# Spreading the late sort passes, making both offsets first, larger groups and narrower clears in a gather, transform and scatter kernel

## The chip, the cores and the metric

The kernel runs on one core of one Trainium2 chip. The metric is the device time of one execution in microseconds. A kernel was run three times or more in its comparison, beside runs of the kernel before on the same chip. A run is called slow when it is over 1.5% above the fastest of the same kernel; only fast runs enter a ratio. Times inside a trace count from the start of the span, which is about 1.7 us shorter than the measured time.

The engines are called PE (the matrix engine), DVE (the vector engine), ACT (the scalar engine) and GpSimd or POOL. PEld is PE's weight load.

## The reference

```python
# nodes 4096 x 256, edges 262144, both weights 256 x 256
self_out = nodes @ w_self
msg = nodes[edges_src] @ w_msg
agg = np.zeros((N, D)); np.add.at(agg, edges_dst, msg)
return self_out + agg
```

## The kernel before

The kernel does not gather rows. It sorts the edges on the chip and then counts, with matrix products of one-hot tiles, how often each pair of source and destination occurs in a narrow band; the counts, multiplied with Y = nodes @ w_msg, give the sums. Until about 164 us it loads and sorts. Then come 2048 chunks of 128 edges. The sort of the second half of the chunks is not finished by then: 32 operations on XL, here called the passes, are done on DVE in between.

For a group of chunks, mostly 64, DVE makes two one-hot tiles, e (128 wide) and d (W = 110 wide). For each it subtracts once (the offset, two inputs, 1024 elements in each partition) and then compares this offset with constants: eight comparisons for e, seven for d.

```python
for nm, val, wid, row in (("e", slo_b, P, jrow), ("d", rel_b, W, drow)):
    o = ohp.tile([P, 32, wid, 2], BF16, name=nm + "_oh", tag=nm, bufs=3)
    ...
        u = ohp.tile([P, 32, JB, 2], I16, name=nm + "_off", tag="off", bufs=2)
        tt(out=u[...], in0=v..., in1=row..., op=ALU.subtract)         # the offset
        for j in range(0, wid, JB):                                   # JB = 16
            w = min(JB, wid - j)
            tss(out=o[:, 0:n // 2, j:j + w, :], in_=u[:, 0:n // 2, 0:w, :],
                scalar=float(-j), op=ALU.is_equal)                    # one comparison
```

PE then counts each chunk with one matmul into a bank of a ring of six in PSUM. A run is one bank filled: it is cleared at both ends by a matmul with zeros, counted into, copied to SBUF by ACT (`atr`), and applied. The last 110 columns of a run belong to its successor. For five of six pairs of runs GpSimd starts a DMA that adds them there (a merge; 163 issues in all, as some merges are split in two). LAG = 46 chunks after its evacuation PE applies the run, and that matmul has to wait for the merge.

```python
def merge(r):
    i, j = r % NAT, (r + 1) % NAT
    ...
        nc.gpsimd.dma_start(
            out=atr[:, b:b + n, 0:W], in_=atr[:, a:a + n, SW:SW + W], accum_op=ALU.add)

def apply_run(r):
    ...
    for t in range(NT):
        nc.tensor.matmul(out=out_ps[:, t, :], lhsT=at[:, t * P:(t + 1) * P], rhs=Y[:, b, :], ...)

    # for each chunk c:
            while nev < NRUN and (evac_at(nev) <= c or c == NCOL - 1):
                evac(nev)
                if nev % 2 == 0 and nev and by_dma(nev - 1):
                    merge(nev - 2)
                todo.append((c + LAG + (SWITCH if nev % NB == 0 else 0), nev))
                ...
            while todo and (todo[0][0] <= c or c == NCOL - 1):
                apply_run(todo.pop(0)[1])
```

## Time and profile before

| Kernel before | |
|---|---|
| median of 3 runs | 481.92 us (481.26 to 483.63) |
| span of the profiled run | 478.6 us |
| busy share PE, DVE, ACT, GpSimd | 79%, 87%, 50%, 41% |
| PE starts chunk 960 | 320.23 us |
| PE starts chunk 2047 | 467.43 us |

```profile
244.54 1.19 POOL L501 DMA_DIRECT2D atr<-atr  x1 [0.26 <-ACT atr L481]
246.21 3.29 POOL L501 DMA_DIRECT2D atr<-atr  x3 [0.48 <-ACT atr L481]
```

d_off begins 0.08 us before the last e comparison ends (244.00 + 2.65 = 246.65), but the d comparisons begin 0.03 us after d_off ends (246.57 + 0.68 = 247.25), because they read it. The three merge issues that started at 246.21 overlap one another and were through 3.29 us later. The longest of all 163 took 1.90 us.

### The profile page before, as it was taken

To read this page: it belongs to the slowest core of one execution; us is meant where nothing else is said; L and a number is where in the kernel's file an instruction comes from. 1 tells how busy PE (TensorE), PEld (TensorE's weight loads), DVE (VectorE), ACT (ScalarE), POOL (GpSimd) and SP (SyncE) were. 2 spreads that over 40 slices of the span, in tenths; PEclk is the share of its full clock that TensorE was granted. 3 is DMA by queue.
4 is the path that set the end of the run, shared out by engine and by line. 5 is a ranking of instruction groups with operands and counts; after the bars stand their busy time and mean duration, and the time that the engine had idled before them with its cause. 6 is when DMAs were issued, how large, how long until landed. Compare 5 with 4: busy or idle time off the path is not lost.

```text
span 478.6 us, 10994 instructions
## 1 busy us (share of the span) xinstructions
PE 378.8 (79%) x4107; PEld 309.2 (65%) x4107; DVE 415.7 (87%) x884; ACT 240.5 (50%) x459; POOL 196.0 (41%) x190
## 2 busy tenths in 40 slices
PE   0009646999872698997887998799999999999994
PEld 0004231655451358996777987699999899999893
DVE  7999999899899999999999998999998687897400
ACT  3100010221282245775555666677776677777771
POOL 4200000000000034665554566577667676776760
PEclk9999986999997699999899899999999999999998
DMA  8794111111000013344243234444535454545451
GB/s 321 118 171 127 25 26 25 27 27 25 14 0 0 0 13 25 28 48 47 24 46 38 28 30 43 49 45 48 54 39 55 38 55 38 57 40 54 38 60 41
DMA packets 66306, 23.78 MB, mean 50 GB/s; under 512 B 52170, under 2 KB 64970, under 8 KB 66250
## 3 DMA queue, kind: packets, MB, share of 16 engines
q0 software_dynamic: 43872, 10.42, 26.8%
q1 hardware_dynamic: 21548, 10.42, 8.3%
q10 hardware_dynamic: 830, 2.20, 1.2%
q8 instruction: 34, 0.56, 0.5%
q14 instruction: 22, 0.18, 0.1%
HBM read 8.92 MB, written 6.30 MB: 32 GB/s over the span
## 4 chain that ended last, share of the span: by engine, by line
DVE 45%; PE 43%; DMA 5%; issue 3%; ACT 2%; POOL 1%; SPq 0%; DVEq 0%; ACTq 0%; POOLq 0%
PE ring L425 17%; DVE XA L749 15%; PE out_ps L524 14%; DVE e_oh L402 9%; DVE d_oh L402 8%; PE warm L786 6%; DVE XS L749 6%; DVE XL L746 4%; PE tp_sw L892 2%; DMA d<-in_edges_dst_dram 2%; DMA atr<-atr 2%; DVE d_off L396 2%; DVE e_off L396 1%; POOL atr L501 1%; PE out_ps L599 1%
## 5 line engine op out<-in xcount | busy, mean ns | idle before, releaser
L501 POOL DMA_DIRECT2D atr<-atr x163 | 187.3, 1265 | 260.0 <-ACT atr L481 257.1
L481 ACT CAST atr<-ring 128x484 bf16<-128x484 f32 x352 | 192.3, 565 | 100.9 <-PE ring L425 80.9
L425 PE MATMUL ring<-d_oh,e_oh 128*128 128x110 bf16 x2048 | 195.6, 215 | 18.4 <-DVE d_oh L402 16.2
L425 PEld LDWEIGHTS <-e_oh 128*128 128x128 bf16 x2048 | 163.8, 98 | 23.6 <-issue 13.9
L524 PE MATMUL out_ps<-Y,atr 128*128 128x256 bf16 x1056 | 171.6, 274 | 1.4 <-DMA atr<-atr 1.4
L402 DVE TENSOR_SCALAR e_oh<-e_off 128x1024 bf16<-128x1024 int16 (+1 forms) x264 | 99.6, 448 | 17.9 <-PE ring L425 15.7
L786 PE MATMUL warm<-zw 128*128 128x512 bf16 x176 | 56.0, 418 | 65.8 <-DVE XA L749 51.4
L749 DVE TENSOR_TENSOR XA<-XA 128x510 f32<-128x510 f32 (+35 forms) x142 | 97.1, 731 | 5.4 <-ACT XA L896 3.7
L524 PEld LDWEIGHTS <-atr 128*128 128x128 bf16 x1056 | 90.5, 98 | 8.2 <-DMA atr<-atr 1.9
L425 PE MATMUL ring<-zer 128*128 128x204 bf16 x352 | 88.3, 251 | 1.4 <-ACT atr L481 1.3
L402 DVE TENSOR_SCALAR d_oh<-d_off 128x1024 bf16<-128x1024 int16 (+3 forms) x231 | 86.2, 443 | 1.1
L786 PEld LDWEIGHTS <-zw 128*128 128x128 bf16 x176 | 16.7, 102 | 101.2 <-issue 55.0
L896 ACT COPY XA<-tp_sw 128x512 f32<-128x512 f32 x24 | 14.2, 592 | 92.5 <-PE tp_sw L892 91.8
L425 PEld LDWEIGHTS <-zer 128*128 128x128 bf16 x352 | 34.4, 98 | 9.8 <-issue 6.0
L749 DVE TENSOR_TENSOR XS<-XS 128x512 f32<-128x512 f32 (+17 forms) x40 | 28.9, 769 | 2.6 <-ACT XS L950 2.0
L746 DVE TENSOR_TENSOR XL<-XL 128x1196 f32<-128x1196 f32 (+15 forms) x32 | 28.1, 918 | 0.3
L892 PEld LDWEIGHTS tp_sw<-XA,id 128*128 128x128 f32 x192 | 22.5, 190 | 4.5 <-issue 2.3
L892 PE MATMUL tp_sw<-XA,id 128*128 128x128 f32 x192 | 23.8, 276 | 1.8 <-DVE XA L749 1.7
L396 DVE TENSOR_TENSOR e_off<-slo_b,jrow 128x1024 int16<-128x1024 int16 (+1 forms) x33 | 21.6, 655 | 0.0
L396 DVE TENSOR_TENSOR d_off<-rel_b,drow 128x1024 int16<-128x1024 int16 (+1 forms) x33 | 21.5, 653 | 0.0
L643 DVE COPY bsum<-ring 1x3 f32<-1x3 f32 x1 | 0.1, 149 | 24.1 <-PE ring L642 24.1
L519 PE MATMUL out_ps<-Y,atr 128*128 128x256 bf16 x65 | 17.6, 272 | 0.0
(104 smaller groups left out, 153.8 us busy)
## 6 DMA issues: line engine op xcount, KB each, us to landing
atr<-atr POOLq DMA_DIRECT2D x123, 55.0 KB, 2.8
out_dram<-o_sb SPq DMA_DIRECT2D x110, 32.0 KB, 1.6
nodes_bf<-in_nodes_dram POOLq DMA_DIRECT2D x1, 2048.0 KB, 16.1
nodes_bf_dram<-nodes_bf SPq DMA_DIRECT2D x1, 2048.0 KB
atr<-atr POOLq DMA_DIRECT2D x40, 27.5 KB, 2.8
s<-in_edges_src_dram ACTq DMA_DIRECT2D x2, 512.0 KB
d<-in_edges_dst_dram SPq DMA_DIRECT2D x2, 512.0 KB, 8.2
XT<-nodes_bf_dram SPq DMA_TRANSPOSE x64, 2.4
```

Of the source, the lines that this page charges most:

```text
L396: tt(out=u[:, 0:n // 2], in0=v.to_broadcast(shp), in1=row[:, 0:JB, :].unsqueeze(1).to_broadcast(shp), op=ALU.subtract,)
L402: tss(out=o[:, 0:n // 2, j:j + w, :], in_=u[:, 0:n // 2, 0:w, :], scalar=float(-j), op=ALU.is_equal,)
L425: mm = nc.tensor.matmul(out=ap, lhsT=lhsT, rhs=rhs, start=start, stop=True, skip_group_check=True,).ins
L481: ins = nc.scalar.copy(out=at[:, 0:SW + W], in_=ring[:, b:b + SW + W]).ins
L501: nc.gpsimd.dma_start(out=atr[:, b:b + n, 0:W], in_=atr[:, a:a + n, SW:SW + W], accum_op=ALU.add)
L519: nc.tensor.matmul(out=out_ps[:, 0, :], lhsT=spill[:, SW:SW + P], rhs=Y[:, b, :], start=False, stop=False, skip_group_check=True,)
L524: nc.tensor.matmul(out=out_ps[:, t, :], lhsT=at[:, t * P:(t + 1) * P], rhs=Y[:, b, :], start=False, stop=(b == NB - 1), skip_group_check=True,
L746: self.defer.append(lambda: self.nc.vector.tensor_tensor(out=out, in0=in0, in1=in1, op=op))
L749: self.nc.vector.tensor_tensor(out=out, in0=in0, in1=in1, op=op),
L786: self.nc.tensor.matmul(out=w[:], lhsT=self.zw[:, 0:P], rhs=self.zw[:], start=True, stop=True).ins
L892: self.nc.tensor.matmul(out=tp[:, g * P:(g + 1) * P], lhsT=self.turned(rots[8 * h + 4 * t + g]), rhs=sel(x)[:, 4 * t + g], start=True, sto ...
L896: self.nc.scalar.copy(out=sel(y)[:, 4 * t:4 * t + 4], in_=tp[:].rearrange("p (g i b) -> p g i b", g=4, b=bb),)
```

## The change

The intent is to balance two regimes. DVE sets the pace while it does the passes, and PE afterwards. The 32 passes are spread over the groups at chunks 192 to 832, two or three a group, in place of those at 256 to 704, four a group. (LATE_FROM and LATE_SUB are where they begin and where they have to be done; LATE_TURN and SHIFT place the transposes of the second half, at a chunk and at a run; LATE_USE, where its places were computed, goes.) Both offsets are made before either comparison, so that no operation reads the one right before it. Groups of 32 become groups of 64 or are compared directly. The clears become 90 columns wide at each end, with a check at the end that this sufficed.

```diff
-GAP = W - 8
+GAP = 90
-SHIFT = 148
-LATE_FROM = 256
-LATE_STEP = 4
-LATE_SUB = 768
-LATE_TURN = 872
-LATE_USE = 960
+SHIFT = 160
+LATE_FROM = 192
+LATE_SUB = 896
+LATE_TURN = 942
...
-    sizes = [8, 8, 16, 32, 32, 32] + [64] * ((NCOL - 128) // 64)
+    sizes = [8, 8, 16, 32] + [64] * 31
...     (split_at: one cut after HALF moved from 256 to 64 chunks)
...     (onehots, shortened)
+        both = []
         for nm, val, wid, row in (("e", slo_b, P, jrow), ("d", rel_b, W, drow)):
-            (offset, then its comparisons)
+            (offset only; for n <= 32 the direct comparison)
+            both.append((o, u, wid))
+        for o, u, wid in both:
+            for j in range(0, wid if u is not o else 0, JB):
+                tss(out=o[...], in_=u[...], scalar=float(-j), op=ALU.is_equal)
...     (loop over chunks)
-                if c == LATE_USE:
-                    late.places()
                 e, d = onehots(c, starts[c])
                 if c >= LATE_FROM:
-                    for _ in range(LATE_STEP):
-                        if rest:
-                            rest.pop(0)()
+                    due = len(ops) * (c + starts[c] - LATE_FROM) // (LATE_SUB - LATE_FROM)
+                    for op in ops[done:due]:
+                        op()
+                    done = max(done, min(due, len(ops)))
                 if c == LATE_SUB:
                     late.bases()
                     ...
+                    late.places()
...     (the check for the fallback: a finer test on bases and first offsets, five tiny operations more)
```

More of the change, by code (lines that the diff above doesn't have):

```diff
@@ L23 @@
 W = 110
-GAP = W - 8
+GAP = 90
 NB = 32
 JB = 16
+MAXG = 64
 HALF = 1024
-SHIFT = 148
-LATE_FROM = 256
-LATE_STEP = 4
-LATE_SUB = 768
-LATE_TURN = 872
-LATE_USE = 960
+SHIFT = 160
+LATE_FROM = 192
+LATE_SUB = 896
+LATE_TURN = 942
 NSEG = 11
@@ L373, in split_vals @@
         tss(out=rel_b[:, c0:c1], in_=vals[:, c0:c1], scalar=7, op=ALU.logical_shift_right)
-    split_at = {0: 64, 64: 512, 512: HALF, HALF: HALF + 256, HALF + 256: NCOL}
-    sizes = [8, 8, 16, 32, 32, 32] + [64] * ((NCOL - 128) // 64)
+    split_at = {0: 64, 64: 512, 512: HALF, HALF: HALF + 64, HALF + 64: NCOL}
+    sizes = [8, 8, 16, 32] + [64] * 31
     assert sum(sizes) == NCOL
     def onehots(c, n):
-        res = []
         if c in split_at:
             split_vals(c, split_at[c])
+        both = []
@@ L384, in onehots @@
         for nm, val, wid, row in (("e", slo_b, P, jrow), ("d", rel_b, W, drow)):
-            o = ohp.tile([P, 32, wid, 2], BF16, name=nm + "_oh", tag=nm, bufs=3)
+            o = ohp.tile([P, MAXG // 2, wid, 2], BF16, name=nm + "_oh", tag=nm, bufs=3)
             v = val[:, c:c + n].rearrange("p (g i) -> p g i", i=2).unsqueeze(2)
-            if n < 32:
-                shp = [P, n // 2, wid, 2]
-                tt(
-                    out=o[:, 0:n // 2], in0=v.to_broadcast(shp),
-                    in1=row[:].unsqueeze(1).to_broadcast(shp), op=ALU.is_equal,
-                )
-            else:
-                u = ohp.tile([P, 32, JB, 2], I16, name=nm + "_off", tag="off", bufs=2)
-                shp = [P, n // 2, JB, 2]
-                tt(
-                    out=u[:, 0:n // 2], in0=v.to_broadcast(shp),
-                    in1=row[:, 0:JB, :].unsqueeze(1).to_broadcast(shp), op=ALU.subtract,
-                )
-                for j in range(0, wid, JB):
-                    w = min(JB, wid - j)
-                    tss(
-                        out=o[:, 0:n // 2, j:j + w, :], in_=u[:, 0:n // 2, 0:w, :],
-                        scalar=float(-j), op=ALU.is_equal,
-                    )
@@ L406, in onehots @@
-            res.append(o)
-        return res
+            u, jb = o, wid
+            if n > 32:
+                u = ohp.tile([P, MAXG // 2, JB, 2], I16, name=nm + "_off", tag=nm + "o", bufs=2)
+                jb = JB
+            shp = [P, n // 2, jb, 2]
+            tt(
+                out=u[:, 0:n // 2], in0=v.to_broadcast(shp),
+                in1=row[:, 0:jb, :].unsqueeze(1).to_broadcast(shp),
+                op=ALU.is_equal if u is o else ALU.subtract,
+            )
+            both.append((o, u, wid))
@@ L410, in line @@
+        for o, u, wid in both:
+            for j in range(0, wid if u is not o else 0, JB):
+                w = min(JB, wid - j)
+                tss(
+                    out=o[:, 0:n // 2, j:j + w, :], in_=u[:, 0:n // 2, 0:w, :],
+                    scalar=float(-j), op=ALU.is_equal,
+                )
+        return [o for o, _, _ in both]
     def line(at, r):
@@ L553 @@
         nev = 0
-        rest = sort.late
+        ops, done = sort.late, 0
         starts = {}
@@ L562 @@
                 c0 = c
-                if c == LATE_USE:
-                    late.places()
                 e, d = onehots(c, starts[c])
                 if c >= LATE_FROM:
-                    for _ in range(LATE_STEP):
-                        if rest:
-                            rest.pop(0)()
+                    due = len(ops) * (c + starts[c] - LATE_FROM) // (LATE_SUB - LATE_FROM)
+                    for op in ops[done:due]:
+                        op()
+                    done = max(done, min(due, len(ops)))
                 if c == LATE_SUB:
-                    assert not rest
+                    assert done == len(ops)
                     late.bases()
@@ L635 @@
     tt(out=v[:], in0=gn[:], in1=gi[:], op=ALU.subtract)
-    stt(out=bad[:], in0=v[:], scalar=float(GAP), in1=bad[:], op0=ALU.is_gt, op1=ALU.add)
+    stt(out=bad[:], in0=v[:], scalar=float(W), in1=bad[:], op0=ALU.is_gt, op1=ALU.add)
+    tt(out=v[:], in0=v[:], in1=dl[:], op=ALU.add)
+    stt(out=bad[:], in0=v[:], scalar=float(SW + GAP), in1=bad[:], op0=ALU.is_gt, op1=ALU.add)
+    tss(out=v[:], in_=v[:], scalar=float(SW), op=ALU.is_ge)
+    stt(out=v[:], in0=dl[:], scalar=float(SW - GAP), in1=v[:], op0=ALU.is_lt, op1=ALU.mult)
+    tt(out=bad[:], in0=bad[:], in1=v[:], op=ALU.add)
     stt(
```

## The prediction

> **What bounds the kernel now.** I read the page's 40 slices first, then a table of busy times by stage, then the waits inside the stages, then the vector engine's timeline. Words used below: a chunk is 128 edges, one matmul into the ring; 2048 chunks are taken in groups, mostly of 64, and for each group DVE (the vector engine) makes two one-hot tiles, e and d; a run is one ring bank, cleared by a matmul, filled, evacuated and applied; the passes are the 32 sort operations on XL that prepare chunks 1024 to 2047.
>
> The 40 slices (11.97 us each):
>
> ```profile
> PE   0009646999872698997887998799999999999994
> DVE  7999999899899999999999998999998687897400
> PEclk9999986999997699999899899999999999999998
> ```
>
> Until slice 13 the kernel sorts, which the change leaves alone. From slice 14 the chunks run. Up to slice 25 DVE has a 9 everywhere and PE has sevens and eights; from slice 26 PE has nines and DVE falls. So there are two regimes. The table of busy times shows it closer (columns: stretch, its length, busy us and count of each engine, granted clock, DMA):
>
> ```profile
> core 0: us, PE busy (x) PEld busy (x) DVE busy (x) ACT busy (x) POOL busy (x), PEclk, DMA share, GB/s
> 209.00:310.00 101.00, 85.47 (x1078) 78.33 (x1076) 97.49 (x223) 61.57 (x116) 57.07 (x50) 0.97 0.40 39
> 320.00:468.00 148.00, 145.29 (x1913) 134.25 (x1911) 111.13 (x268) 107.42 (x202) 102.06 (x89) 1.00 0.48 47
> ```
>
> First row: DVE is busy 97%, PE 85%. Second row: PE 98%, DVE 75%. The waits say the same, first for 200 to 308 us, then for 310 to 450 us (us in total, times, longest):
>
> ```profile
> PE ring L425 <- DVE d_oh L402: 13.8, 8, 3.1
> DVE gn L633 <- DMA kn<-kd: 1.7, 1, 1.7
> ```
>
> ```profile
> DVE e_oh L402 <- PE ring L425: 15.7, 11, 3.4
> ```
>
> Early, PE waits for the one-hots; late, DVE waits for PE to give a one-hot buffer back. Counting the ring matmuls off the timeline: group 960 starts on PE at 320.23 us, chunk 2047 at 467.43, so 17 groups take 147.2 us, 8.66 each. DVE had group 960 ready at 316.97. The end of the program is therefore the time at which PE can start group 960 plus a stage that PE sets, plus a tail of 11.2 us (478.6 - 467.43).
>
> What DVE does before then, in its own timeline (start, us, what):
>
> ```profile
> 280.59 2.65 DVE L746 TENSOR_TENSOR XL<-XL 128x528 f32<-128x528 f32 x4
> 283.16 0.68 DVE L396 TENSOR_TENSOR e_off<-slo_b,jrow 128x1024 int16<-128x1024 int16 x1
> 283.95 2.88 DVE L402 TENSOR_SCALAR e_oh<-e_off 128x1024 bf16<-128x1024 int16 x8
> 286.75 0.68 DVE L396 TENSOR_TENSOR d_off<-rel_b,drow 128x1024 int16<-128x1024 int16 x1
> 287.46 2.88 DVE L402 TENSOR_SCALAR d_oh<-d_off 128x1024 bf16<-128x1024 int16 x7
> ```
>
> A group is 7.2 us: from e_off to the end of d_oh the 13 groups 128 to 896 took 95.4 us, less the 1.7 us wait for kn in one of them, over 13. Four passes behind a group cost another 2.5 to 5.1. So a step with passes was 9.4 to 12.6 us against PE's 8.66, and the steps without them (before chunk 256, after 704) were shorter than PE's. In the timeline an operation that reads the one just before it starts 0.11 us after its end (e_oh after e_off) or 0.03 us (d_oh after d_off); one that doesn't starts 0.08 us before the end of its predecessor.
>
> [...] 512 elements of e_oh took 309 ns, 1024 took 462 on average and about 0.35 us a step where nothing disturbed them. [...] The trace has 249 ns at 204 columns and 215 at 110, 0.36 ns a column, so 9. [...] Here the two longest pauses of PE (3.46 us from start to start before 228.1, 3.03 before 260.9) are followed by windows with a granted clock of 0.91 to 0.92 and 0.83[...].
>
> **The change, part by part.**
> 1. Spread: 32 passes go from eight groups (256 to 704, four each) to eleven (192 to 832, two or three each). The DVE work before group 960 is the same, 26.9 us of step time. What changes is who waits: DVE's steps become about 7 + 2.5 = 9.5 us, close to PE's. PE's idle gaps shrink from 3 us to about 1[...].
> 2. Offsets first: e_off, d_off, e_oh, d_oh. Two dependent starts vanish: 0.11 + 0.08 and 0.03 + 0.08, 0.30 us. Part of the 0.11 is probably the wait for the buffer, which stays, so I take 0.24 us: a group is 6.96 us.
> 3. Groups: the two groups of 32 at 64 and 96 took 9.08 us of DVE (173.92 to 183.00) and become one of 64, 6.96 us: 2.1 saved. The group of 32 at chunk 32 is now made by two direct comparisons. One over 2048 elements took 1.22 us and one over 1760 1.07; twice the elements, an estimate, 2.3 + 2.0 us, against 4.1 now. Nothing either way.
> 4. Bases, subtraction and places move together behind group 896: 2.4 + 1.5 us as before. The wait for kn (1.7 us) should vanish, as about 2.9 us of other DVE work now lies between. The wider test adds 5 tiny operations of 0.17 us, some 0.6 us with overlaps.
> 5. Clears: 352 matmuls of 180 columns in place of 204[...]. It counts only where PE is the bound: 17 groups with 11 runs each[...].
>
> Sum for DVE. Group 64 starts at 174.1 (as now, 173.92, plus 0.2). 15 groups to the end of group 960: 15 x 6.96 = 104.4. Passes 26.9, the split of values at 512 0.5, bases to places 3.9, test 0.6. 174.1 + 136.3 = 310.4; I take 311.0, as the passes' ops summed singly come out 1.2 us higher. PE: group 896 is ready at about 299.5 and takes 8.55 us plus 1.5 for the eight transposes of the late half, so it is done at 309.6 and waits for group 960 until 311.0. Before: 320.23. Gain 9.2 us. Behind it DVE's steps of about 7 are shorter than PE's 8.55, so PE stays the bound and the stage shrinks only by the clears' 1.9. Total 11.1: 481.9 - 11.1 = 470.8 us.
>
> Of the 9.2, 6.0 is DVE being done earlier (316.97 to 311.0). The other 3.2 is that PE is no longer late behind DVE there: the transposes and the slot waits of the late half, which delayed PE at 301 to 312 us (group 832 took 10.2 us), now fall in a group behind which PE would wait anyway.
>
> **The rivals.**
> A. DVE's work before group 960 is what counts, and spreading does not shrink it. If offsets-first and merging save nothing, DVE has group 960 ready at 316.97 - 1.7 + 0.6 = 315.9; the gain is 4.3 + 1.9 and the time 475.7. For it: DVE is at 97% in the stage either way. Against it: the dependent starts are plain in the timeline.
> B. PE becomes the bound over the whole stretch, as DVE's tensor_scalar steps get shorter. They range from 0.27 to 0.85 us, so some of them are held up by something. PE alone would start group 960 at 189 + 13 x 8.55 + 1.5 = 301.7, and the time would be 461.5. Against it: 6.96 + 2.5 is longer than 8.55.
> C. The late half turns late: transposes now at chunks 928 and 942, and the one-hots of 1024 need them. PE is at 942 at about 307, ScalarE takes 0.7 us, DVE asks at about 311: a slack of 3 us. If it were lost, DVE would wait, but PE still has group 960 to chew on, so it costs 0 to 3 us, up to 474.
> D. The looser test fails on these data, and the slow general path runs: far slower. I took the edges from the reference, sorted them exactly and applied the new test: largest step between neighbouring bases 96 (limit 110), largest first offset in a run 69 (limit 90), smallest last offset 298 (limit 284). The network sorts almost so; I give it 2%.
>
> **Range and chances.** DVE's group time is the large uncertainty: 0.2 us either way over 15 groups is 3 us. PE's group time of 8.55 with 0.1 either way is 1.7 us. Before's three runs scatter over 2.4 us. I take 466.5 to 475.5. The limit of 2% is 472.3, only 1.5 us from my number, so faster 0.62, same 0.36, slower 0.02.
>
> **What would show it.** Group 960 starts on PE at 309 to 313 us; DVE's e_oh follows d_off with an overlap, and a group takes about 7.0; waits of PE for d_oh many but short (under 2 us); the wait for kn gone; clears near 240 ns; 8.5 us a group after 960. The prediction is wrong if groups still take 7.2 us, if PE waits for vals, or if PE's stage after 960 grows.

For the clears it takes 1.9 us, which no trace shows. By the trace's 0.36 ns a column (249 ns at 204 columns, 215 at 110), 24 columns are 9 ns, and the 187 clears (17 groups with 11 runs each) 1.7 us.

## More of the kernel before

From the page, its slices, and the group of its merge issues (busy us, mean ns of one, then its idle time):

```profile
POOL 4200000000000034665554566577667676776760
L501 POOL DMA_DIRECT2D atr<-atr x163 | 187.3, 1265 | 260.0 <-ACT atr L481 257.1
```

From slice 16 on (slices count from 0) GpSimd is mostly 50 to 70% busy with nothing but these issues, and what ends its idle time is ACT, which has evacuated a run. This held nobody up: PE hardly ever waited for a merge. From the waits of the whole run (us in total, times, longest):

```profile
PE out_ps L524 <- DMA atr<-atr: 1.4, 3, 1.0
```

Now a stretch of the timeline, first DVE's, then GpSimd's (start, us, engine and line, operation, output and inputs, how many; in brackets the idle time before it):

```profile
244.00 2.65 DVE L402 TENSOR_SCALAR e_oh<-e_off 128x1024 bf16<-128x1024 int16 x7
246.57 0.68 DVE L396 TENSOR_TENSOR d_off<-rel_b,drow 128x1024 int16<-128x1024 int16 x1
247.28 2.44 DVE L402 TENSOR_SCALAR d_oh<-d_off 128x1024 bf16<-128x1024 int16 x7
```

The chain that ended last, by engine:

```profile
DVE 45%; PE 43%; DMA 5%; issue 3%; ACT 2%; POOL 1%; SPq 0%; DVEq 0%; ACTq 0%; POOLq 0%
```

## The result, and the profile after

The changed kernel took 487.77 us, the median of four runs (486.88 to 490.17), against 482.75 us (481.26 to 483.63, four runs) before. The ratio is 1.0115, with a 95% interval from 1.0068 to 1.0162: 1.2% slower, inside the 2% that count as the same. The result is correct. A ratio here and below is the mean time of one kernel's fast runs over that of the other's of the same rounds, so it is not quite the ratio of the medians quoted.

The slices of the page after (12.2 us each):

```profile
PE   0009636989871886978888999977999999999994
DVE  8998999899899999999968999766868779786400
POOL 4200000000000057786868666768676676776660
PEclk9999885999996798988989999998999999999998
```

DVE has lost its row of nines from 244 us on (its 21st digit), as was wanted, but PE has not gained them: it shows a 6 at 183 to 195 us and two sevens at 317 to 342 us. Of the three engines shown only GpSimd has become busier over the whole span (46% in place of 41). The busy times by stretch (columns as in the prediction's table; the first stretch is shown for this kernel, the other two answer to the rows of before):

```profile
180.00:250.00 70.00, 57.22 (x674) 51.07 (x674) 65.72 (x144) 37.23 (x68) 54.56 (x34) 0.91 0.36 32
```

```profile
209.00:310.00 101.00, 89.98 (x1113) 80.25 (x1111) 92.76 (x228) 62.11 (x117) 72.69 (x53) 0.95 0.41 40
320.00:478.00 158.00, 148.67 (x1951) 136.22 (x1949) 110.24 (x276) 111.10 (x209) 110.66 (x89) 0.99 0.45 45
```

From 209 to 310 us neither DVE (92.76 of 101) nor PE (89.98) is full now. GpSimd was busy for 72.69 us with 53 issues, before for 57.07 with 50. The number of merges is unchanged, so each takes longer:

```profile
L498 POOL DMA_DIRECT2D atr<-atr x163 | 217.6, 1620 | 239.5 <-ACT atr L478 237.1
```

The mean is 1620 ns where it was 1265, the longest 6670 where it was 1901, and 19 issues are over 2 us where none was. The waits of the whole run show who pays:

```profile
PE out_ps L521 <- DMA atr<-atr: 17.5, 10, 3.9
DVE e_oh L400 <- PE ring L422: 32.4, 18, 4.3
DVE slo_b L371 <- ACT vals L311: 7.4, 2, 6.9
PE ring L422 <- DVE d_oh L400: 1.9, 1, 1.9
```

PE's wait for one-hots has nearly gone, as intended. In its place PE waits 17.5 us for merged runs, and 10.5 of them in the stretch from 170 to 250 us. DVE, now ahead, waits for PE to give buffers back. One such wait in the timeline, for DVE, GpSimd and PE in turn:

```profile
207.59 0.68 DVE L391 TENSOR_TENSOR e_off<-slo_b,jrow 128x1024 int16<-128x1024 int16 x1
208.19 0.68 DVE L391 TENSOR_TENSOR d_off<-rel_b,drow 128x1024 int16<-128x1024 int16 x1
208.80 2.77 DVE L400 TENSOR_SCALAR e_oh<-e_off 128x1024 bf16<-128x1024 int16 x8
211.48 2.40 DVE L400 TENSOR_SCALAR d_oh<-d_off 128x1024 bf16<-128x1024 int16 x7
213.80 1.22 DVE L748 TENSOR_TENSOR XL<-XL 128x1024 f32<-128x1024 f32 x1
```

```profile
209.11 6.31 POOL L498 DMA_DIRECT2D atr<-atr  x2 [0.31 <-ACT atr L478]
```

```profile
215.87 0.39 PE L521 MATMUL out_ps<-Y,atr 128*128 128x256 bf16 x2 [2.46 <-DMA atr<-atr]
```

Each DVE line begins before the one above it ends. The fifteen comparisons are one chain without a gap from 208.80 to 213.88 us. The merge issue that begins at 209.11, 0.31 us into the chain, lasts until 214.20 (the first of the two on the line; 5.09 us alone), when the chain is over and a pass has begun. An undisturbed issue takes 1.19 us. The merge lands at 215.82, and PE, which has stood for 2.46 us, goes on at 215.87.

The chain that ended last contains GpSimd now, with 13% (before 1%), and DMAs with 8% (before 5%), of which the page puts 6% down to the merges (before 2%):

```profile
PE 43%; DVE 22%; POOL 13%; issue 10%; DMA 8%; ACT 2%; SPq 0%; POOLq 0%; DVEq 0%; ACTq 0%
```

Where the time came from is plainest in the moments at which PE starts certain chunks. The last column anticipates experiment 1, the changed kernel with the old order of offsets.

| chunk | before | after | after, old order |
|---|---|---|---|
| 192 | 198.37 | 204.04 | 199.87 |
| 448 | 239.24 | 250.83 | 236.55 |
| 896 | 311.97 | 313.74 | 302.75 |
| 960 | 320.23 | 324.92 | 315.49 |
| 1024 | 329.04 | 339.56 | 324.14 |
| 2047 | 467.43 | 477.26 | 462.55 |

By chunk 448 the changed kernel is 14.3 us behind its old-order sister. It regains 4.9 us by chunk 960 (PE has work in store while DVE is ahead) and loses 6.0 again in the group from 960 to 1024. There the late transposes, at chunk 942 on PE, come late because PE is late; DVE waits 6.9 us for `vals`, and PE then waits for DVE.

### The profile page after: what moved, and what is told of

It reads as the page before. It is cut to its first block, busy times and chain, and to the rows that moved or that the text cites.

```text
span 488.4 us, 10958 instructions
## 1 busy us (share of the span) xinstructions
PE 382.8 (78%) x4098; PEld 309.8 (63%) x4107; DVE 404.7 (83%) x857; ACT 240.8 (49%) x459; POOL 226.3 (46%) x190
## 4 chain that ended last, share of the span: by engine, by line
PE 43%; DVE 22%; POOL 13%; issue 10%; DMA 8%; ACT 2%; SPq 0%; POOLq 0%; DVEq 0%; ACTq 0%
PE ring L422 17%; PE out_ps L521 15%; DVE XA L751 15%; POOL atr L498 13%; DMA atr<-atr 6%; DVE XS L751 6%; PE warm L788 5%; PE tp_sw L894 2%; DMA d<-in_edges_dst_dram 2%; PE out_ps L516 1%; PE out_ps L510 1%; PE out_ps L596 1%; ACT XA L898 1%; ACT atr L478 1%; PE tp_sw L307 0%
## 5 line engine op out<-in xcount | busy, mean ns | idle before, releaser
L498 POOL DMA_DIRECT2D atr<-atr x163 | 217.6, 1620 | 239.5 <-ACT atr L478 237.1
L521 PE MATMUL out_ps<-Y,atr 128*128 128x256 bf16 x1056 | 173.8, 276 | 18.5 <-DMA atr<-atr 17.5
L422 PEld LDWEIGHTS <-e_oh 128*128 128x128 bf16 x2048 | 161.5, 98 | 16.3 <-issue 6.6
L400 DVE TENSOR_SCALAR e_oh<-e_off 128x1024 bf16<-128x1024 int16 x248 | 94.2, 450 | 32.5 <-PE ring L422 32.4
L422 PE MATMUL ring<-zer 128*128 128x180 bf16 x352 | 85.3, 242 | 1.5 <-ACT atr L478 1.3
L400 DVE TENSOR_SCALAR d_oh<-d_off 128x1024 bf16<-128x1024 int16 (+1 forms) x217 | 78.8, 431 | 0.0
L391 DVE TENSOR_TENSOR d_off<-rel_b,drow 128x1024 int16<-128x1024 int16 x31 | 21.1, 680 | 0.0
L391 DVE TENSOR_TENSOR e_off<-slo_b,jrow 128x1024 int16<-128x1024 int16 x31 | 21.1, 680 | 0.0
L516 PE MATMUL out_ps<-Y,atr 128*128 128x256 bf16 x65 | 17.8, 274 | 0.5 <-issue 0.4
```

Of the source, the lines that this page charges most:

```text
L391: tt(out=u[:, 0:n // 2], in0=v.to_broadcast(shp), in1=row[:, 0:jb, :].unsqueeze(1).to_broadcast(shp), op=ALU.is_equal if u is o else ALU.s ...
L422: mm = nc.tensor.matmul(out=ap, lhsT=lhsT, rhs=rhs, start=start, stop=True, skip_group_check=True,).ins
L498: nc.gpsimd.dma_start(out=atr[:, b:b + n, 0:W], in_=atr[:, a:a + n, SW:SW + W], accum_op=ALU.add)
L516: nc.tensor.matmul(out=out_ps[:, 0, :], lhsT=spill[:, SW:SW + P], rhs=Y[:, b, :], start=False, stop=False, skip_group_check=True,)
```

## The experiments

Twelve kernels were run. My theory: the rests that the old order left on DVE, where an operation had to wait for the result right before it, were the moments at which GpSimd could go on with an issue; the unbroken chain of fifteen comparisons holds it, merges land late and PE waits. The rivals: the larger lead of DVE, the spread, or the new clears or groups cost the time in themselves.

This table gives what the profiled run of each showed: PE's start of chunk 960, the time from there to chunk 2047, mean and longest issue of GpSimd, and PE's waits of `out_ps` for merges. For e11 the profiled run was a slow one.

| run | ratio to before | 960 starts | 960 to 2047 | issue mean / longest, ns | waits for merges, us |
|---|---|---|---|---|---|
| before | 1 | 320.23 | 147.19 | 1265 / 1901 | 1.4 |
| after | 1.0115 | 324.92 | 152.35 | 1620 / 6670 | 17.5 |
| e1 old order | 0.9860 | 315.49 | 147.07 | 1274 / 1901 | 0.8 |
| e2 before, offsets first | 1.0041 | 317.70 | 150.36 | 1520 / 6372 | 13.3 |
| e3 tiny between | 0.9890 | 312.63 | 154.01 | 1475 / 6247 | 7.5 |
| e4 lag 60 | 0.9825 | 310.00 | 147.97 | 1550 / 6665 | 7.2 |
| e5 tiny dependent | 0.9911 | 312.92 | 152.27 | 1448 / 3925 | 6.2 |
| e6 old order, wide clears | 0.9911 | 314.74 | 150.09 | 1272 / 1889 | 3.8 |
| e7 before, spread only | 0.9865 | 316.62 | 148.64 | 1262 / 1873 | 1.9 |
| e8 passes between | 0.9752 | 313.30 | 148.18 | 1355 / 3866 | 4.5 |
| e9 before, groups only | 1.0005 | 319.12 | 147.63 | 1275 / 1963 | 1.0 |
| e10 = e8 with lag 54 | 0.9744 | 311.21 | 147.14 | 1350 / 3522 | none |
| e11 offsets first from 960 | 1.0123 | slow run | slow run | slow run | slow run |
| e12 four rests more | 1.0025 | 323.16 | 151.12 | 1261 / 1876 | 2.4 |

### 1. The changed kernel with the old order (e1)

```diff
             both.append((o, u, wid))
-        for o, u, wid in both:
             for j in range(0, wid if u is not o else 0, JB):
```

> The changed kernel with the one-hots made in the old order (e_off, e_oh, d_off, d_oh), all else as changed. Theory 1 (GpSimd is locked out): with both offsets first the 15 comparisons of a group run as one chain on VectorE with no break, and a merge that GpSimd begins to issue inside it is held until the chain ends (up to 6.7 us); the merges land late and PE waits for them. Then here the mean issue time falls from 1620 to about 1265 ns as in the kernel before, PE's wait for the merges from 17.5 to under 4 us, and the time to 470 to 476 us. Theory 2 (pace): the merges were always only just in time, hidden because PE waited for one-hots; whatever frees PE lays them bare. Then the waits for merges stay above 12 us and the time stays at 483 to 488 us.

It took 476.0 us (475.45 to 478.4), ratio 0.986 (0.9803 to 0.9918) to before, against 1.0115 with both offsets first. The order alone is worth 2.6% or 12 us. The issues of GpSimd are those of before (minimum, median and longest of one in ns, from the view of its line), PE waits for one-hots again instead of merges, and in the stretch from 180 to 250 us PE did 838 matmuls, not 674:

```profile
L497 POOL DMA_DIRECT2D atr<-atr x163: 888/1192/1901, 175.1 to 459.1; - x163
```

```profile
180.00:250.00 70.00, 63.59 (x838) 58.97 (x838) 68.74 (x145) 45.61 (x84) 42.54 (x38) 0.98 0.40 37
```

GpSimd spent 42.54 us on 38 issues here and 54.56 on 34 in the changed kernel, where moreover the clock granted to PE fell to 0.91 from 0.98.

### 2. The kernel before with both offsets first (e2)

```diff
-                u = ohp.tile([P, 32, JB, 2], I16, name=nm + "_off", tag="off", bufs=2)
+                u = ohp.tile([P, 32, JB, 2], I16, name=nm + "_off", tag=nm + "o", bufs=2)
...
-                for j in range(0, wid, JB):   # comparisons at once
+                both.append((o, u, wid))
...
+        for o, u, wid in both:
+            for j in range(0, wid, JB):       # comparisons after both offsets
```

> The kernel before with both offsets first as its only change. Theory 1: GpSimd's mean issue time rises from 1265 to 1450 to 1650 ns, PE waits 8 us or more for merges, and the time is 483 to 490 us. Theory 2: GpSimd's mean stays under 1300 ns; DVE saves some 0.24 us a group, and the time falls to 476 to 480 us.

It took 485.05 us (480.96 to 486.54), ratio 1.0041 (0.9983 to 1.0099): not to be told from the kernel before. The mechanism is there without spread, groups or clears. The longest issue is 6372 ns, and

```profile
PE out_ps L526 <- DMA atr<-atr: 13.3, 8, 4.3
```

while PE's wait for d one-hots fell to 1.3 us. Chunk 960 started 2.5 us sooner, the stage behind it took 3.2 us longer: a gain given back.

### 3. A tiny independent operation between the comparisons (e3)

```diff
-        for o, u, wid in both:
+        for i, (o, u, wid) in enumerate(both):
+            if i and u is not o:
+                tt(out=tiny[:], in0=val[:, c:c + 8], in1=val[:, c:c + 8], op=ALU.subtract)
```

> The changed kernel with one tiny two-input operation (8 elements a partition, on a scratch tile, nothing depends on it) between the e and the d comparisons of each group: the chain of 15 becomes 8 and 7. Theory 1: if a two-input operation lets GpSimd in, as the trace suggests, no issue takes longer than about 4 us, the mean is under 1400 ns, and the time is 470 to 477 us; if only a dependent start does, nothing changes (487). Theory 2: nothing changes, or 3 us longer for the added operations.

It took 478.85 us (476.99 to 479.54), ratio 0.989 (0.9833 to 0.9946). An eight-element operation won back 2.2% of the time, but not all, and theory 1's expectation missed in all its three numbers. The longest issue in the stretch with passes was 2.4 us; between 310 and 350 us, where chains follow on one another, one took 6247 ns. An operation that merely follows on without a wait does not reliably let GpSimd in.

### 4. More time between evacuation and application (e4)

```diff
-LAG = 46
+LAG = 60
```

> The changed kernel with each run applied 60 chunks after its evacuation in place of 46, so a merge has about 1.9 us more. Both theories: PE's wait for merges falls by half or more, and the time falls to 473 to 481 us if that wait is what costs. Theory 1: GpSimd's mean issue time stays at about 1600 ns; theory 2: it is 1265 to 1600. If the time stays at 487 us, the waits for merges are not what made the change slow.

The result is wrong (not a number): with this lag one of the paced stores, of 22 rows, was never issued, nine in place of ten. One store of 22 KB fewer is little against a span of 470 us (those of 32 KB took a median of 1.5 us from issue to landing in this run), so I use the time, with that reservation: 474.23 us (471.53 to 476.78), ratio 0.9825 (0.9765 to 0.9884). GpSimd's issues are as long as ever (mean 1550, longest 6665 ns), but the waits for merges fell:

```profile
PE out_ps L521 <- DMA atr<-atr: 7.2, 3, 3.3
```

So long issues cost where PE has to wait for what they start; whether they cost anything else is not shown, as the old order was not run with this lag. The rival that the lead of DVE costs time in itself is out: order and lead are those of the changed kernel, and the time is 13.5 us less. (By the interval, whether this run is over 2% faster than before is unclear.)

### 5. One rest, by a tiny dependent operation (e5)

```diff
+            if i and u is not o:
+                z = both[0][0][:, 0, P - 4:P, :]          # written by the last e comparison
+                tt(out=tiny[:], in0=z, in1=z, op=ALU.subtract)
```

> As the run with a tiny operation between the e and d comparisons, but the tiny operation now reads what the last e comparison wrote, so VectorE has to finish the chain before it starts (some 0.1 us of rest, once a group). In that run the stretch without passes (310 to 350 us) still had issues of up to 6.2 us, so an operation that merely follows on did not let GpSimd in. If it is the rest that does: no issue over about 3.5 us in any stretch, a mean of 1270 to 1400 ns, PE's wait for merges under 5 us, and 472 to 477 us. If it is not the rest but the order of e_off and d_off that matters: as that run, a mean near 1475 ns and 478 to 480 us.

It took 478.09 us (477.76 to 479.32), ratio 0.9911 (0.9863 to 0.9959), 1 us above what I expected. The longest issue is 3925 ns and PE's waits for merges are 6.2 us, both a little above what I expected too; the mean (1448) stayed above that of before. One rest in fifteen comparisons bounds the delay and does not remove it.

### 6. The old order with wide clears (e6)

```diff
-GAP = 90
+GAP = W - 8
# and the old order of e1
```

> The changed kernel in the old order and with the clears at 204 columns again (GAP 102). [...] expected 1.5 to 3.5 us slower than the old-order run, so 477.5 to 479.5 us. If clears cost nothing: 476.

It took 478.02 us (477.74 to 479.1), ratio 0.9911 (0.9864 to 0.9958), against 0.986 for e1 with narrow clears. The difference is 0.5% or about 2.4 us; the intervals overlap, and the two ran on different chips. The clears themselves, in this kernel and in the changed one:

```profile
L421 PE MATMUL ring<-zer 128*128 128x204 bf16 x352 | 87.9, 250 | 1.4 <-ACT atr L477 1.3
```

```profile
L422 PE MATMUL ring<-zer 128*128 128x180 bf16 x352 | 85.3, 242 | 1.5 <-ACT atr L478 1.3
```

### 7. The spread alone (e7)

```diff
 # the kernel before with only:
-SHIFT = 148 ... LATE_FROM = 256, LATE_STEP = 4, LATE_SUB = 768, LATE_TURN = 872, LATE_USE = 960
+SHIFT = 160 ... LATE_FROM = 192, LATE_SUB = 896, LATE_TURN = 942; places() with bases()
```

> The kernel before with the spread of the passes as its only change (192 to 896, the later turn, bases and places together; groups, order and clears as before). The prediction's rival A without merging and clears gives 4.3 us less 2.1 for the groups: 2 to 4 us faster than before, 478 to 481 us. GpSimd's issues stay at about 1265 ns. If the late turn of the second half costs, it is not faster.

It took 476.75 us (474.9 to 478.16), ratio 0.9865 (0.9814 to 0.9915): 5.9 us by the medians, more than expected. Chunk 960 started 3.6 us sooner. The rival that the spread costs time in itself is refuted. Alone it is as good as everything but the order together (e1), within the intervals.

### 8. Offsets first, with the passes between the comparisons (e8)

```diff
+        if 192 <= c < 896:
+            compare(*both[0], n)
+            between()                  # this group's two or three passes
+            compare(*both[1], n)
# other groups: the old order
```

> An attempt to keep the gain of both offsets first without the long chain: in the groups with passes (192 to 832) both offsets first, but the passes, fp32 two-input operations of 0.7 to 1.4 us, between the e and the d comparisons; in all other groups the old order. Theory 1: the longest issue is about 3.5 us, the mean under 1400 ns, PE starts group 960 some 3 us sooner than in the old-order run (315.5), and the time is 471 to 474.5 us. If chains of 8 still lock GpSimd out enough to hold PE: 476 to 480.

It took 471.07 us (469.93 to 474.37), ratio 0.9752 (0.9703 to 0.9801), and is correct. Whether it is over 2% faster than before is unclear by the interval. It keeps the offsets first where they save DVE time, breaks the chain with work that has to be done anyway, and has the old order where PE is the bound.

### 9. The groups alone (e9)

```diff
-    sizes = [8, 8, 16, 32, 32, 32] + [64] * ((NCOL - 128) // 64)
+    sizes = [8, 8, 16, 32] + [64] * 31
...
-            if n < 32:
+            if n <= 32:
```

> The kernel before with its two groups of 32 at chunks 64 and 96 made one of 64, and the group at 32 compared directly, as its only change. VectorE bounds that stretch, and 2.1 us of its work go: 0 to 2.5 us faster than before. If PE, which now has to wait for a whole group of 64, loses more than that: up to 2 us slower.

It took 481.36 us (479.65 to 484.98), ratio 1.0005 (0.9965 to 1.0046). No gain shows, and one of 2.1 us (0.44%) lies outside the interval.

### 10. The better version (e10)

```diff
 # e8 with:
-LAG = 46
+LAG = 54
+            while c == NCOL - 1 and stores:
+                nc.sync.dma_start(*stores.pop(0))
```

> The run with the passes between the e and d comparisons, with runs applied 54 chunks after their evacuation in place of 46 (and what stores are left issued at the end, so that none is lost as in the run with 60). That run's PE still waited 4.5 us for merges; half of it or more should go: 468 to 471 us, over 2% faster than the kernel before. If it is no faster than 471, those waits lay beside other waits.

It took 470.31 us (468.7 to 471.59, six runs), ratio 0.9744 (0.9719 to 0.9769) against 482.4 before: faster, also beyond 2%, and correct. No wait of PE for merges is left. From 209 to 310 us DVE is full and PE not far from it, with a granted clock of 1.00:

```profile
209.00:310.00 101.00, 93.15 (x1236) 86.16 (x1234) 99.69 (x240) 71.11 (x130) 70.87 (x59) 1.00 0.46 45
```

PE did 1236 matmuls here, against 1078 before and 1113 in the changed kernel. Against e8 the gain is within the scatter.

### 11. Offsets first only from chunk 960 (e11)

```diff
+            if c < 960:
+                compare(o, u, wid, n)
+        for o, u, wid in both if c >= 960 else ():
+            compare(o, u, wid, n)
```

> The changed kernel with the old order up to group 896 and both offsets first from group 960 on. Theory 1 in its sharper form: GpSimd is held only while VectorE runs on without a rest, which after 960 is the case until VectorE is three buffers ahead of PE (some four groups); from then on its waits for PE give GpSimd its turns. So long issues (over 3 us) only between 305 and 350 us, a mean of about 1300 to 1450 ns, 2 to 6 us of waits for merges, and 477 to 482 us against 476 of the old order throughout. If the chain of 15 by itself locks GpSimd out, rest or not, long issues go on to 450 us and the time is 482 or more.

Its fast runs took 485.41, 488.93 and 490.48 us, ratio 1.0123 (1.0078 to 1.0169). The expectation missed. I had sharpened the theory to say that a chain behind a rest is safe, and it is not. The profiled run (496.23 us, clock 0.939) is a slow one, so no time is taken from it; that it contains issues of 3.5 to 6.7 us between 314 and 364 us, two of them begun 1.44 and 1.73 us into a chain that followed a rest, led to the counts below. The order in the second half alone is enough to lose what the rest of the change gains.

### 12. Four rests in fifteen comparisons (e12)

```diff
+                if k % 4 == 0:            # before comparisons 0, 4, 8 and 12
+                    z, t = (...) if k == 0 else (last, tiny)
+                    tt(out=t[:], in0=z, in1=z, op=ALU.subtract)
```

> The changed kernel with four rests in each chain of 15 comparisons: a tiny operation that reads what the operation before it wrote, ahead of the comparisons 0, 4, 8 and 12. In the traces so far, of the first issues that GpSimd began inside a chain of 15 that started after a rest, the 21 that began up to 1.33 us after the start were not held and the 4 from 1.44 us on were held to its end. If that is the rule (an issue gets in up to about 1.3 us after a rest of VectorE and waits for the next rest otherwise), then with a rest every 1.3 us no issue is long: longest about 2.0 us, mean 1265 to 1330 ns, PE's wait for merges under 4 us; VectorE pays some 0.8 us a group for the four operations and rests, so a group is 7.0 to 7.4 us and the time 474 to 479 us. If length of the chain and not rest is what counts, long issues (over 3 us) stay and the time is 482 or more.

GpSimd was freed entirely: its longest issue took 1876 ns, and PE waited 2.4 us for merges. Yet the time was 485.52 us (483.51 to 487.19), ratio 1.0025 (0.9962 to 1.0088), where I had expected 474 to 479.

```profile
L507 POOL DMA_DIRECT2D atr<-atr x163: 841/1192/1876, 173.9 to 470.4; - x163
```

```profile
PE ring L431 <- DVE d_oh L407: 16.9, 9, 3.5
```

A group without a wait for PE took DVE 7.2 to 8.4 us, not 7.0 to 7.4, and PE waits 16.9 us for one-hots, as before (16.2). DVE had group 960 ready at 323.10 us and PE started it at 323.16: here DVE is the bound, and it pays for the four operations, the rests and GpSimd's turns. How much each of them costs was not separated.

### What the traces give as a rule, and where it ends

I took all traces but that of e12 and sorted the merge issues that were the first to begin inside a chain of comparisons, with no other issue under way when the chain or the issue began (0.03 us allowed).

- Chains of seven or eight that begin after a wait for their offset (gap of up to 0.2 us): 135 issues, none over 1.9 us. Yet eight of them that began 1.27 to 1.76 us into the chain took 1.27 to 1.82 us, not 1.19, and ended 0.31 us after its last comparison, as a held issue does. So short chains hold too, but there is little left of them to wait for.
- Chains of seven or eight that follow on without a rest (nearly all in e3, e5, e8 and e10): 46 issues, 13 of them over 2 us, the longest 3.02 us.
- Chains of fifteen that begin after a longer rest: the 20 issues that began up to 1.33 us into the chain were not held; the three that began 1.44, 1.73 and 2.04 us in were held to its end. The first two of these three are from the slow trace of e11. (The expectation of e12 counts 21 and 4: with an earlier issue allowed to reach 0.12 us into the chain.)
- Chains of fifteen that follow on without a rest, as in the changed kernel: 14 of 20 issues were held to the end, one that began only 0.31 us into the chain among them. Why six were let in stays open.

Where an earlier issue ran across the start of a chain of fifteen behind a rest, 1.44 us is no limit: of ten issues that began that late or later, five were let in, up to 2.76 us into the chain, and five were held. So a rest is followed by a time in which an issue gets in, and a long chain leaves the more to wait for; a full rule this is not.

While an issue runs beside the comparisons, a step of DVE takes up to 0.77 us; while the issue of 209.11 us is held, every step is 335 to 338 ns. That DVE shows the full pace exactly then is why I call the issue held and not merely slow. Whether DVE stops and goes on inside a step of 0.77 us can't be seen in the trace.

Two other issues of the changed kernel began at 328.69 and 329.43 us, just before the chain from 329.68 to 334.76, and ended behind it, at 334.86 and 336.10, the second with 6.67 us the longest of all. They did not get in between comparisons that stepped every 0.335 us.

## Why the prediction was wrong

I predicted 470.8 us (466.5 to 475.5) and the time was 487.77 us. In spans: 467.5 was predicted and 488.4 measured in the profiled run, 20.9 us more (it was the slowest of the four runs; the others had 485.1 to 486.2). The start of chunk 960 was predicted at 311.0 us and came at 324.92: 13.9 us. The stage behind it was predicted at 145.3 us and took 152.35: 7.0 us. The tail was right.

**The step that failed** is part 2: "Offsets first: e_off, d_off, e_oh, d_oh. Two dependent starts vanish: 0.11 + 0.08 and 0.03 + 0.08, 0.30 us." They did vanish, and more came of it than I took: a group in which GpSimd is held throughout takes DVE 6.3 us, not 6.96. But the step counted the rests as DVE's loss alone. They were GpSimd's turns. With them gone, issues are held for up to a whole chain, merges land late, and PE waits. Put back into the changed kernel, the old order brings 12 us (e1); put into the kernel before, the new order brings the long issues (e2); with more time to land, long issues cost less (e4); with rests put back, they are gone (e12), though these rests did not win the time back. This much is shown.

With it failed the prediction's path, in which PE "is done at 309.6 and waits for group 960 until 311.0". It was PE that came late. The last comparisons of group 960 on DVE and PE's first matmul of that group, in the changed kernel and then in e2:

```profile
311.95 2.53 DVE L400 TENSOR_SCALAR d_oh<-d_off 128x1024 bf16<-128x1024 int16 x7
324.92 0.31 PE L422 MATMUL ring<-d_oh,e_oh 128*128 128x110 bf16 x3
```

```profile
303.89 2.45 DVE L405 TENSOR_SCALAR d_oh<-d_off 128x1024 bf16<-128x1024 int16 x7
317.70 0.32 PE L427 MATMUL ring<-d_oh,e_oh 128*128 128x110 bf16 x3
```

DVE had the group ready at 314.48 and 306.34 us (in the kernel before at 316.97), so offsets first did save DVE time, in e2 even 10.6 us; PE began it 10.4 and 11.4 us after it was ready. With the old order (e1) PE began at 315.49 what was ready at 315.43.

The prediction held the clue. Rival B noted that the comparisons "range from 0.27 to 0.85 us, so some of them are held up by something", and did not ask by what. Laid beside GpSimd's timeline, the slow steps are those under a merge issue (in the kernel before all 133 comparisons of 1024 elements that took over 0.45 us; the 81 beside no issue took at most 0.43). No rival named GpSimd, as its share of 41% looked harmless.

No run shows by what means the comparisons hold an issue. The trace shows what ran beside it: the comparisons (tensor_scalar) step every 0.335 us for 1024 elements, the offsets (tensor_tensor) every 0.60, and the held issue shown above began 0.31 us into the chain of comparisons and ended 0.32 us after the last of them, with a pass (tensor_tensor) running.

**Rival C** happened, in another way. "If PE waits for vals" was named as what would make the prediction wrong, with a slack of 3 us and a cost of 0 to 3. DVE did wait 6.9 us for vals, and chunk 1024 started 14.6 us after 960 in place of 8.65 in e1. But this follows from PE being late: in e1, with the same late turn, DVE waited 0.3 us for vals, and chunk 1024 came in time.

**Rival A** (475.7 us, group 960 ready on DVE at 315.9) is what the rest of the change does: e1 took 476.0, and DVE had that group ready at 315.43.

**Sizes of the other parts.** The spread was right in direction and too small: rival A's working leaves it 4.3 us before chunk 960 if nothing else saves time, and the spread alone brought 5.9 us of time (e7), 3.6 of them at the start of 960 in its profiled run. The groups, 2.1 us in the sum, showed no gain (e9); a group of 64 lets PE begin only when all of it is compared (chunk 64 starts at 181.29 us after, at 179.12 before), which probably takes back what DVE saves. The clears, 1.9 us, measured about 2.4 (e6 against e1), with overlapping intervals. The looser check passed, so rival D did not happen, and the wait for kn did go.

**What would have shown the prediction right** was mostly there: e_oh follows d_off with an overlap (208.80 against 208.19 + 0.68), waits for d_oh shrank to one of 1.9 us, clears are at 242 ns. None of these is the end of the program. The two that are, group 960 at 309 to 313 us and 8.5 us a group behind it, both failed, and of its signs of being wrong, PE's stage after 960 did grow (147.19 to 152.35 us).

**Two readings** in it are loose, without consequence for the failure. Group 832 took 10.57 us on PE (301.40 to 311.97), not 10.2. And the two pauses of PE before the lower clock are 3.15 and 2.81 us long when counted as idle time; from start to start the first is 3.40 us, not 3.46. That a pause lowers the clock is not shown: one of 2.33 us before 249.77 us was followed by a clock of 1.00 (250 to 260 us).

## What to carry to other kernels

Before closing gaps on one engine, look at which other engine is at work in these gaps, and what waits for it: a rest of 0.1 us on DVE can be what lets GpSimd go on with the issue of a DMA (issues of 1274 ns on average with such rests in e1, of 1620 ns without). A long unbroken chain of DVE operations is better broken with work that has to be done anyway (e8, e10: ratios 0.9752 and 0.9744) than with rests, which the bounding engine pays (e12: 1.0025). And an engine's busy share says little about how late its results may come; ask how much slack lies between its issue and the instruction that needs it, and give it more where there is room (LAG 60 brought 13.5 us to the changed kernel, e4).
